# Seven products for a sixth pair of up chunks in each MLP, with sums of weight quarters made during attention

## The chip, the cores and the metric

One core of one Trainium2 chip runs one program. The metric is the device time of one execution in microseconds (us); lower is better. A profile of one execution gives the engines' instructions, their waits and the DMA packets. The engines are PE (TensorE, matmuls), DVE (VectorE), ACT (ScalarE), POOL (GpSimd) and SP (SyncE, which here only issues DMAs); a "q" behind a name is the engine's instruction queue.

## What is computed

A trunk of two layers works on 256 tokens of width 2048, all in float32. Layer 0 is causal attention with forget gates (FoX, 16 heads of 128), layer 1 is a mixture of three dilated windows (8 heads). Each mixer is followed by an MLP with a hidden width of 8192:

```
x = x + mixer(rms_norm(x) ; w_in, w_out)
h = rms_norm(x)
a = relu(h @ w_up)            # w_up 2048 x 8192
x = x + (a * a) @ w_down      # w_down 8192 x 2048
```

The weights, some 400 MB, are read from DRAM once in each run.

## The kernel before

**Matmuls.** To keep float32 accuracy, each operand is split into a rounded part `hi` and a rest `lo` (type fp32r), and each product is three matmuls (hi by hi, hi by lo, lo by hi; L447 to L449 in `product_steps`, L1138 to L1140 in `slot_steps`). A matmul is 128x128 by 128x512. A weight matrix is cut into chunks of 512 columns, and a chunk into row blocks of 128.

**A unit of weights.** Two row blocks of one chunk, 128x1024 floats or 512 KB, are one unit. SP loads it into one of five `raw` buffers (`load`, L373), ACT casts it to `wh` (L398), DVE subtracts to get `wl` (L399, both in `split_part`), and PE multiplies it with both halves of the tokens: 2 row blocks x 2 token tiles x 3 = 12 matmuls. There are five buffers of `wh` and five of `wl`, so units are split up to five ahead of PE. A raw buffer is loaded again when DVE has split its unit.

**The order.** Everything is written as coroutines in class `Jobs`. `product_steps` calls `jobs.tick()` behind each row block (a *step* below is one tick; one row block is 6 matmuls). A job that says `yield n` goes on n ticks later, `yield key` waits until that key is reached, and `clear(n)` is n or n+1 ticks, whichever ends on the right parity. The order in which instructions are written is the order in which each engine runs them; `pin` fixes it. So a chain is placed by counting ticks, and an engine that reaches an instruction too early waits there with all that is behind it.

**Stages.** FoX attention: 12 chunks of `fox_w_in`, then 4 of `fox_w_out`. MLP "n1". Dilated attention: 16 chunks of `dil_w_in`, 4 of `dil_w_out`. MLP "n3". During the attention chunks, heads run beside the products: `qk_chain` (norms, a transpose through DRAM blocks, scaling), `fox_head` and `dil_head` (scores, softmax, the transpose of the probabilities by `p_turned` through DRAM, `pv`).

**An MLP** has four blocks b of the hidden width, of four up chunks n each. `UP_ALONE` lists up chunks that are ordinary products; chunks 0 and 1 of block 0 are ordinary as well. Behind the up chunks of a block come its four down chunks. Counted in units of ordinary work, an MLP has 22 chunks x 8 = 176 units.

**Wide pairs.** The remaining up chunks go in pairs (b, n), (b, n+1) as 2x2 blocks: two row blocks by two chunks are four quarters B11, B12, B21, B22, the two token tiles by two row blocks are A11 to A22, and the product is formed with seven products in place of eight, by sums of quarters on both sides (`PRODUCTS`). The sums of tokens are made once for each MLP (`token_sums`). For each of the 8 pairs `pr` of row blocks, three *slots* are woven between ordinary units, and one more slot for two `pr` together:

- what 0, "crossed": the quarters off the diagonal, as they are (2 products, 6 matmuls)
- what 1, "differences": `sd` = crossed minus B22 (2 products)
- what 2, "sums": `v` (2 products)
- what 3, "rows": B21 of two `pr`, for the eighth matrix of partial sums (2 products for two `pr`)

Each slot is a unit of 512 KB that ACT casts and DVE subtracts as any other. DVE also makes `sd` and `v` (L395 128x1024; L401 and L402, 128x512 each) in `split_part`. Two loads of 512 KB feed slots 0 to 2, one load feeds a slot 3. `WIDE_AT` says behind which ordinary unit of the MLP each slot of each pair comes; a slot is also one tick. `wide_chain` then adds the six banks of partial sums (L1100 to L1109, one ACT copy and six DVE operations of 128x512), applies relu and square, and `turn_up` transposes through DRAM and splits into `aTh`, `aTl` (tags of four buffers each), which the down chunks read. Those two tags also hold the attention outputs `oT`.

The five pairs are (1,0), (2,0), (2,2), (3,0), (3,2).

Of the kernel before, what the change touches and what calls it, by code (L numbers as in the profile page):

```python
# [9 lines left out]
F32 = mybir.dt.float32  # L10
# [7 lines left out]
P = 128  # L18
D = 2048
S = 256  # L20
NT = S // P
NC = 512
# [97 lines left out]
def trunk(ctx: ExitStack, tc, x, fox_w_in, fox_b_f, fox_q_gain, fox_k_gain, fox_w_out, dil_w_in,  # L120
# [168 lines left out]

    def add_slot(w, c, what, pr):  # L290

        r = pr * RAW_SUB * P
        if what == 3:
            units.append((len(plan), "rows"))
            plan.append([((slice(0, RAW_SUB), slice(0, NC)),
                          w[r:r + 2 * RAW_SUB * P, c:c + NC].rearrange("(c q p) n -> p c q n", p=P, q=RAW_SUB)[:, :, 0])])
            return
        if what == 0:
            woven["at"] = len(plan)
            for first, by in ((0, NC), (NC, -NC)):  # L300
                corner = w[r:r + P, c + first:c + first + NC]
                rows, columns = corner.ap
                crosswise = bass.AP(corner.tensor, corner.offset, [rows, [rows[0] * P + by, RAW_SUB], columns])
                plan.append([((slice(0, RAW_SUB), slice(0, NC)), crosswise)])
        units.append((woven["at"] + 1, ("crossed", "differences", "sums")[what]))
# [17 lines left out]
    def add_mlp(l):  # L323
        woven["count"] = 0
        for at, (b, n, what, pr) in wide_slots():
            woven["due"].setdefault(at, []).append((mlp_w_up[l], b * D + n * NC, what, pr))
# [38 lines left out]
    def load():  # L365
        i = state["raw"]
        if i >= len(plan):
            return
        t = wpool.tile([P, RAW_SUB, NC], F32, tag="raw", name=f"raw{i}", bufs=RAW_BUFS)
        for (k, columns), src in plan[i]:  # L370
            hold(t)
            for rows in [slice(x, x + 1) for x in range(RAW_SUB)] if i == 1 else [None]:
                nc.sync.dma_start(t[:, k if rows is None else rows, columns], src if rows is None else src[:, rows])  # L373
        raws.append(t)
        state["raw"] += 1
# [39 lines left out]

    def in_turn(w, apart=NC // 2):
# [673 lines left out]
    def wide_chain(banks, tag, b, n, aT):  # L1092
# [34 lines left out]

    def slot_steps(tag, banks, what, pr, then):

        hi, lo = splits[used[0]]  # L1130
        for bank, i, a, of in [(0, i, 4, pr + i) for i in range(2)] if what == 3 else [(*x, pr) for x in PRODUCTS[what]]:
            wh, wl = (in_turn(w[:, i, :]) for w in (hi, lo))
            if a < 4:
# [13 lines left out]
    def mlp(tag, **after):  # L1147
        aTs = [{} for b in range(4)]
        banks = []

        def one(b, n, what, pr):
            if pr == 0 and what in (0, 2):
                pools = ((ps_acc, f"acc{1 - turn['only']}"),) if what else ((ps_tp, "tp"), (ps_sc, "sc"))
                banks[2 * what:] = [pool.tile([P, NC], F32, tag=of, name=f"wide_{tag}_{b}_{n}_{of}{i}")
                                    for pool, of in pools for i in range(2)]
# [9 lines left out]
            slot_steps(tag, banks, what, pr, then)  # L1165

# [95 lines left out]

    tag = "n0"
    for j in range(4):
        qT, kT = zip(*(heads_pairs(f"f{j}_{i}", i) for i in range(2)))
# [54 lines left out]
```

## Time and profile before

| | |
|---|---|
| median of 3 runs | 2084.48 us (2082.59 to 2084.88) |
| the profiled execution | 2084.9 us, its span 2083.2 us |
| PE busy / DVE busy / ACT busy | 2076.8 / 1714.9 / 1305.8 us |
| POOL busy | 275.2 us |
| DMA | 539.04 MB, mean 259 GB/s |
| core's granted TensorE clock | 1.00 |

The span runs from the first instruction to the last; the 1.7 us outside it are start and end of the execution. Busy time of an engine is the union of its instructions' durations. PE's matmuls are pipelined: a matmul that lasts 379 ns is followed by the next long before its end, so the pace is read from the starts, not from the durations. "DMA share" is the mean share of time in which packets were under way on the 16 DMA engines; packets that overlap on one engine can take it over 1.

### The profile page before, as it was taken

How to read it: one execution, taken by the hardware profiler on the slowest of the kernel's cores; microseconds unless marked ns; L12 is line 12 of the kernel's file. 1: busy time of each engine (PE TensorE's matmuls, PEld its weight loads, DVE VectorE, ACT ScalarE, POOL GpSimd, SP SyncE). 2: the span in 40 equal slices, each digit the busy share in tenths (PEclk: the TensorE clock that was granted, in tenths of full speed). 3: DMA queues.
4: the chain of work that ended last, by engine and by line, in shares of the span. 5: the costliest groups of instructions: out<-in, count | busy, mean ns of one | idle time of the engine just before them, and what ended most of it. 6: DMA issues, size and time to landing. Idle time of an engine off the chain costs nothing.

```text
span 2083.2 us, 28968 instructions
## 1 busy us (share of the span) xinstructions
PE 2076.8 (100%) x9835; PEld 1818.5 (87%) x9835; DVE 1714.9 (82%) x2183; ACT 1305.8 (63%) x1825; POOL 275.2 (13%) x398
## 2 busy tenths in 40 slices
PE   9999999999999999999999999999999999999999
PEld 7888888888888888888888888888888888888888
DVE  6888876898989889888668787766998898899874
ACT  6665654866666667564656565556766676666662
POOL 2000000011212111120010010000113031212120
PEclk9999999999999999999999999999999999999999
DMA  7888887888988898897877876877889888898885
GB/s 254 259 259 260 262 248 212 267 285 262 268 281 269 262 296 269 267 291 247 279 242 229 250 239 210 260 212 237 262 272 272 278 276 265 276 287 276 265 280 165
DMA packets 357205, 539.04 MB, mean 259 GB/s; under 512 B 43752, under 2 KB 144448, under 8 KB 357056
## 3 DMA queue, kind: packets, MB, share of 16 engines
q1 hardware_dynamic: 334624, 507.41, 76.8%
q0 software_dynamic: 22016, 29.38, 6.2%
q8 instruction: 77, 1.26, 0.3%
q10 hardware_dynamic: 416, 0.39, 0.1%
q14 instruction: 72, 0.59, 0.1%
HBM read 484.09 MB, written 40.39 MB: 252 GB/s over the span
## 4 chain that ended last, share of the span: by engine, by line
PE 97%; ACT 1%; DMA 1%; DVE 1%; issue 0%; SPq 0%; ACTq 0%; DVEq 0%
PE acc L448 26%; PE acc L447 26%; PE acc L449 25%; PE wide_n_tp L1139 2%; PE wide_n_tp L1140 2%; PE wide_n_tp L1138 2%; PE wide_n_sc L1139 2%; PE wide_n_acc L1140 2%; PE wide_n_acc L1139 2%; PE wide_n_sc L1140 2%; PE wide_n_sc L1138 2%; PE wide_n_acc L1138 2%; PE sc_d L798 0%; DMA raw<-in_fox_w_in_dram 0%; ACT room_n L552 0%; ACT wh L398 0%
## 5 line engine op out<-in xcount | busy, mean ns | idle before, releaser
L399 DVE TENSOR_TENSOR wl<-raw,wh 128x1024 fp32r<-128x1024 f32 (+1 forms) x763 | 919.5, 1214 | 308.5 <-ACT wh L398 299.3
L398 ACT CAST wh<-raw 128x1024 fp32r<-128x1024 f32 (+1 forms) x763 | 787.2, 1046 | 505.5 <-PE acc L449 368.7
L447 PE MATMUL acc<-wh,hT_n 128*128 128x512 f32 x1280 | 486.7, 380 | 0.4 <-ACT hT_n L628 0.2
L448 PE MATMUL acc<-wl,hT_n 128*128 128x512 f32 x1280 | 485.6, 379 | 0.5 <-DVE wl L399 0.5
L449 PE MATMUL acc<-wh,hT_n 128*128 128x512 f32 x1280 | 485.4, 379 | 0.0
L449 PEld LDWEIGHTS acc<-wh,hT_n 128*128 128x128 f32 x1280 | 241.9, 189 | 34.8 <-DVE hT_n L629 0.4
L448 PEld LDWEIGHTS acc<-wl,hT_n 128*128 128x128 f32 x1280 | 242.1, 189 | 34.6 <-DVE wl L399 2.1
L447 PEld LDWEIGHTS acc<-wh,hT_n 128*128 128x128 f32 x1280 | 242.1, 189 | 34.3 <-ACT hT_n L628 1.2
L447 PE MATMUL acc<-wh,aTh_n1a 128*128 128x512 f32 x512 | 194.0, 379 | 0.0
L448 PE MATMUL acc<-wl,aTh_n1a 128*128 128x512 f32 x512 | 194.0, 379 | 0.0
L449 PE MATMUL acc<-wh,aTl_n1a 128*128 128x512 f32 x512 | 194.0, 379 | 0.0
L447 PE MATMUL acc<-wh,aTh_n3a 128*128 128x512 f32 x480 | 181.9, 379 | 0.0
L448 PE MATMUL acc<-wl,aTh_n3a 128*128 128x512 f32 x480 | 181.9, 379 | 0.0
L449 PE MATMUL acc<-wh,aTl_n3a 128*128 128x512 f32 x480 | 181.9, 379 | 0.0
L994 POOL DMA_DIRECT2D x<-y_n x96 | 84.7, 1331 | 479.9 <-ACT y_n L993 421.4
L398 ACT CAST wh<-sd 128x1024 fp32r<-128x1024 f32 x80 | 84.1, 1051 | 99.4 <-DVE sd L395 77.6
L398 ACT CAST wh<-v 128x1024 fp32r<-128x1024 f32 x80 | 84.1, 1051 | 54.3 <-PE acc L449 42.7
L448 PEld LDWEIGHTS acc<-wl,aTh_n1a 128*128 128x128 f32 x512 | 96.8, 189 | 13.8
L447 PEld LDWEIGHTS acc<-wh,aTh_n1a 128*128 128x128 f32 x512 | 96.8, 189 | 13.7
L449 PEld LDWEIGHTS acc<-wh,aTl_n1a 128*128 128x128 f32 x512 | 96.8, 189 | 13.7
L449 PEld LDWEIGHTS acc<-wh,aTl_n3a 128*128 128x128 f32 x480 | 90.7, 189 | 12.9
L447 PEld LDWEIGHTS acc<-wh,aTh_n3a 128*128 128x128 f32 x480 | 90.7, 189 | 12.9
(665 smaller groups left out, 3227.7 us busy)
## 6 DMA issues: line engine op xcount, KB each, us to landing
raw<-in_mlp_w_up_dram SPq DMA_DIRECT2D x296, 512.0 KB, 4.9
raw<-in_mlp_w_down_dram SPq DMA_DIRECT2D x256, 512.0 KB, 5.0
raw<-in_dil_w_in_dram SPq DMA_DIRECT2D x192, 256.0 KB, 3.6
raw<-in_fox_w_in_dram SPq DMA_DIRECT2D x94, 512.0 KB, 4.7
raw<-in_fox_w_out_dram SPq DMA_DIRECT2D x32, 512.0 KB, 4.9
raw<-in_dil_w_in_dram SPq DMA_DIRECT2D x32, 512.0 KB, 5.4
raw<-in_dil_w_out_dram SPq DMA_DIRECT2D x32, 512.0 KB, 4.4
x<-y_n POOLq DMA_DIRECT2D x96, 128.0 KB, 6.4
```

The source lines that it names most:

```text
L398: nc.scalar.copy(hi[:, part, :], raw[:, part, :])
L399: nc.vector.tensor_sub(lo[:, part, :], raw[:, part, :], hi[:, part, :].bitcast(F32))
L447: nc.tensor.matmul(acc[t], ah[:, tok], hi, start=first, stop=False)
L448: nc.tensor.matmul(acc[t], ah[:, tok], lo, start=False, stop=False)
L449: nc.tensor.matmul(acc[t], al[:, tok], hi, start=False, stop=last)
L994: nc.gpsimd.dma_start(xt[n][:, t, h * HC:h * HC + HC], y, accum_op=ALU.add)
L1138: nc.tensor.matmul(banks[bank], ah, wh, start=what < 3 and of == 0, stop=False, **alone)
L1139: nc.tensor.matmul(banks[bank], ah, wl, start=False, stop=False, **alone)
L1140: nc.tensor.matmul(banks[bank], al, wh, start=False, stop=of == KC // 2 - 1, **alone)
```

## The change

Three things.

1. **A sixth pair.** (1,2) joins `WIDE`, `UP_ALONE[1]` becomes empty, and an MLP has 20 ordinary chunks, 160 units. `WIDE_AT` is written anew: the first pair's slots lie behind units 15 to 37, and from then on a pair begins every 18 units (39, 57, 75, 93, 111), its eight `pr` two units apart. Before, the pairs began at 15, 45, 71, 98 and 122.

2. **Sums ahead.** A new job, `sums_ahead(l, start)`, runs beside the attention chunks of its layer: for each (b, n, pr) in `AHEAD[l]` it loads crossed and diagonal quarters (two loads of 512 KB, on SP), makes the differences and the sums with four DVE operations (one 128x1024, three 128x512), and stores both to DRAM (`kept`, two stores of 512 KB, on POOL). `AHEAD[0]` has ten row block pairs (the eight of pair (1,0), one of (2,0), one of (3,0)); `AHEAD[1]` has sixteen (the eight of (1,0) and two each of (1,2), (2,0), (2,2), (3,0)). In the MLP, such a `pr` is three plain loads (crossed from the weights, both sums from `kept`), and DVE makes no `sd` and `v` for it. The work tiles are one buffer each of the tags `aTh` and `aTl`.

3. **The first copy of `wide_chain` moves.** The chain is now started when slot 0 of the last `pr` is done; it copies P1 at once and waits for a key, "pieces", reached behind slot 2 of the last `pr`. The banks are kept in a dictionary by pair.

```diff
-WIDE = ((1, 0), (2, 0), (2, 2), (3, 0), (3, 2))
-WIDE_AT = ((15, 19, 23, 27, 31, 34, 37, 39, 41, 42, 42, 43), (45, 47, 50, 53, 55, 58, 61, 63, 66, 67, 67, 68),
-           (71, 74, 77, 79, 82, 85, 87, 90, 93, 93, 94, 95), (98, 101, 103, 106, 109, 111, 114, 117, 119, 119, 120, 120),
-           (122, 125, 127, 130, 133, 135, 138, 141, 143, 143, 144, 145))
-UP_ALONE = ((2, 3), (2, 3), (), ())
+WIDE = ((1, 0), (1, 2), (2, 0), (2, 2), (3, 0), (3, 2))
+WIDE_AT = ((15, 18, 20, 23, 26, 28, 31, 33, 35, 36, 36, 37),
+           *(tuple(at + x for x in (0, 2, 4, 6, 8, 10, 12, 14, 15, 16, 16, 16)) for at in range(39, 112, 18)))
+AHEAD = tuple([(1, 0, pr) for pr in range(KC // 2)] + more for more in (
+    [(2, 0, 4), (3, 0, 0)], [(*pair, pr) for pair in WIDE[1:5] for pr in (2, 5)]))
+UP_ALONE = ((2, 3), (), (), ())
...
-    def add_slot(w, c, what, pr):
+    def add_slot(w, c, what, pr, ahead=None):
...
+        if ahead is not None:
+            units.append((len(plan), "rows"))
+            plan.append([(whole, (ahead, what - 1) if what else crosswise(w, r, c, -NC))])
+            return
...
+    def sums_ahead(l, start):
+
+        yield start
+        diagonal, crossed = (act.tile([P, RAW_SUB, NC], F32, tag=f"aT{x}", name=f"ahead_{l}_{x}", bufs=KC // 4) for x in "hl")
+        for i, (b, n, pr) in enumerate(AHEAD[l]):
+            at = mlp_w_up[l], pr * RAW_SUB * P, b * D + n * NC
+            move(crossed, crosswise(*at, -NC))
+            move(diagonal, crosswise(*at, NC))
+            yield clear(5)
+            first, second = (crossed[:, x, :] for x in range(2))
+            q11, q22 = (diagonal[:, x, :] for x in range(2))
+            nc.vector.tensor_sub(crossed, crossed, q22.unsqueeze(1).to_broadcast([P, RAW_SUB, NC]))
+            yield 1
+            nc.vector.tensor_add(q22, q22, first)
+            nc.vector.tensor_add(q22, q22, second)
+            yield 1
+            nc.vector.tensor_sub(q11, q11, q22)
+            kept[l, b, n, pr] = [dram.tile([P, RAW_SUB, NC], F32, tag=f"kept{x}", name=f"kept_{l}_{i}_{x}", bufs=sum(map(len, AHEAD)))
+                                 for x in range(2)]
+            nc.gpsimd.dma_start(kept[l, b, n, pr][0], crossed)
+            yield 1
+            nc.gpsimd.dma_start(kept[l, b, n, pr][1], diagonal)
+            yield 5
...
     def wide_chain(banks, tag, b, n, aT):
...
+        p1 = by_column(banks[0])
+        nc.scalar.copy(c12, p1)
+        yield (key, "pieces", n)
         p1, p3, p7, p5, p6, p4 = (by_column(x) for x in banks)
-        nc.scalar.copy(c12, p1)
-        yield 1
         nc.vector.tensor_sub(c12, c12, p6)
...
             def then():
+                if what == 0 and pr == KC // 2 - 1:
+                    jobs.spawn(wide_chain(banks, tag, b, n, aTs[b]))
                 if what == 2 and pr == KC // 2 - 1:
-                    jobs.spawn(wide_chain(list(banks), tag, b, n, aTs[b]))
+                    jobs.reach((f"{tag}a{b}", "pieces", n))
...
     tag = "n0"
+    jobs.spawn(sums_ahead(0, 20))
...
     mlp("n1", then=normed("n2", KC))
+    jobs.spawn(sums_ahead(1, 4))
     dilated("n2")
```

A `pr` made ahead has its two quarters the other way round in the buffer, which `slot_steps` takes into account (`turned`).

More of the change, by code (lines that the diff above doesn't have):

```diff
@@ L288, in add, with crosswise @@
             woven["count"] += 1
-    def add_slot(w, c, what, pr):
+    def crosswise(w, r, c, by):
+        corner = w[r:r + P, c + (0 if by > 0 else NC):c + (0 if by > 0 else NC) + NC]
+        rows, columns = corner.ap
+        return bass.AP(corner.tensor, corner.offset, [rows, [rows[0] * P + by, RAW_SUB], columns])
+    kept = {}
+    def add_slot(w, c, what, pr, ahead=None):
         r = pr * RAW_SUB * P
@@ L297, in add_slot @@
             return
+        whole = (slice(0, RAW_SUB), slice(0, NC))
+        if ahead is not None:
+            units.append((len(plan), "rows"))
+            plan.append([(whole, (ahead, what - 1) if what else crosswise(w, r, c, -NC))])
+            return
         if what == 0:
             woven["at"] = len(plan)
[L300 to L304, printed above, removed]
+            for by in (NC, -NC):
+                plan.append([(whole, crosswise(w, r, c, by))])
         units.append((woven["at"] + 1, ("crossed", "differences", "sums")[what]))
@@ L1126, in wide_chain, with slot_steps @@
         yield from turn_up(squared(first, tiles[1]), key, n, aT, (tag, "free", b - 1, n))
-    def slot_steps(tag, banks, what, pr, then):
+    def slot_steps(tag, banks, what, pr, then, turned=False):
         hi, lo = splits[used[0]]
         for bank, i, a, of in [(0, i, 4, pr + i) for i in range(2)] if what == 3 else [(*x, pr) for x in PRODUCTS[what]]:
-            wh, wl = (in_turn(w[:, i, :]) for w in (hi, lo))
+            wh, wl = (in_turn(w[:, 1 - i if turned else i, :]) for w in (hi, lo))
             if a < 4:
@@ L1159, in then @@
             def then():
+                if what == 0 and pr == KC // 2 - 1:
+                    jobs.spawn(wide_chain(banks, tag, b, n, aTs[b]))
                 if what == 2 and pr == KC // 2 - 1:
-                    jobs.spawn(wide_chain(list(banks), tag, b, n, aTs[b]))
+                    jobs.reach((f"{tag}a{b}", "pieces", n))
                 if what == 3 and pr == KC // 2 - 2:
                     jobs.reach((f"{tag}a{b}", "crossed", n))
-            slot_steps(tag, banks, what, pr, then)
+            slot_steps(tag, banks, what, pr, then, what == 2 and (b, n, pr) in AHEAD[int(tag == "n3")])
         jobs.spawn(token_sums(tag))
```

12 lines of the change are left out of this document (9 added, 3 removed).

## Prediction, before the run

> **What bounds the kernel now.** First the page: the span, the busy times, the chain that ended last.
>
> ```profile
> span 2083.2 us, 28968 instructions
> PE 2076.8 (100%) x9835; PEld 1818.5 (87%) x9835; DVE 1714.9 (82%) x2183; ACT 1305.8 (63%) x1825; POOL 275.2 (13%) x398
> PE 97%; ACT 1%; DMA 1%; DVE 1%; issue 0%; SPq 0%; ACTq 0%; DVEq 0%
> ```
>
> PE is idle for 2083.2 - 2076.8 = 6.4 us in all, so the time is the number of matmuls times their pace. The pace is in PE's timeline inside MLP n1 (the first of 16 matmuls in a row and the last):
>
> ```profile
> 699.67 0.38 PE L447 MATMUL acc<-wh,aTh_n1a 128*128 128x512 f32 x1
> ...
> 702.91 0.38 PE L1138 MATMUL wide_n_tp<-wh,hT_n 128*128 128x512 f32 x1
> ```
>
> 15 starts lie in 3.24 us: 0.216 us for each matmul, a step (6) is 1.30 us, an ordinary unit (12) 2.59 us. All that PE can gain is fewer matmuls; all that it can lose is waiting for an engine that now hides behind it. So the next views are the stages' windows (columns: length, then busy time of PE, PEld, DVE, ACT, POOL with counts, clock, DMA share, GB/s), of FoX, MLP n1 and dilated attention, then three short ones with much DMA:
>
> ```profile
> 50.00:250.00 200.00, 200.00 (x980) 176.56 (x979) 164.38 (x286) 119.37 (x194) 10.74 (x6) 1.00 0.85 258
> 517.00:918.00 401.00, 401.00 (x1859) 350.87 (x1858) 358.74 (x368) 264.67 (x318) 79.97 (x123) 1.00 0.88 274
> 1020.00:1340.00 320.00, 320.00 (x1557) 282.33 (x1556) 240.13 (x349) 190.19 (x278) 24.10 (x13) 1.00 0.79 242
> 10.00:20.00 10.00, 9.74 (x49) 7.82 (x50) 8.23 (x15) 7.07 (x15) 0.83 (x3) 1.00 1.05 393
> 915.00:945.00 30.00, 30.00 (x141) 26.27 (x140) 25.40 (x32) 20.05 (x27) 13.09 (x22) 1.00 0.97 310
> 620.00:640.00 20.00, 20.00 (x94) 17.50 (x94) 18.70 (x21) 15.39 (x21) 8.95 (x17) 1.00 0.95 317
> ```
>
> DVE is busy for 82% of FoX, 89% of the MLP's weave, 75% of the dilated stretch. ACT's largest share is 66%, so it has room. What DVE and the SP queue waited for says whether these are near their limits (us, times, longest; the first two rows are FoX, 28 to 228 us, the third is SP over the span):
>
> ```profile
> DVE wl L399 <- ACT wh L398: 29.9, 35, 1.9
> DVE bias L882 <- DMA bias<-negc: 3.1, 2, 2.5
> SPq L373 <- DVE wl L399: 804.9, 437, 4.9
> ```
>
> SP waits for a free raw buffer for 805 us: the loads run as fast as units are used up, so the rates of the windows above are demand, not a ceiling.
>
> **The change part by part.**
>
> *The sixth pair.* Two ordinary chunks are 2 x 16 row blocks x 2 token tiles x 3 = 192 matmuls. A wide pair is 8 `pr` x 3 slots x 6, and 4 slots of 6: 168. 24 are saved in each MLP, 48 in all, x 0.216 = **10.4 us off PE**. There is no cover here: PE is the path.
>
> *DVE in the denser weave.* What operations take on DVE when nothing holds them is read from start to start:
>
> ```profile
> 652.47 1.23 DVE L395 TENSOR_TENSOR sd<-raw,raw 128x1024 f32<-128x1024 f32 x1
> 653.61 1.22 DVE L399 TENSOR_TENSOR wl<-raw,wh 128x1024 fp32r<-128x1024 f32 x1
> 654.75 0.68 DVE L401 TENSOR_TENSOR v<-raw,sd 128x512 f32<-128x512 f32 x1
> 655.46 0.69 DVE L402 TENSOR_TENSOR v<-raw,v 128x512 f32<-128x512 f32 x1
> 656.07 1.22 DVE L399 TENSOR_TENSOR wl<-sd,wh 128x1024 fp32r<-128x1024 f32 x1
> 657.21 1.22 DVE L399 TENSOR_TENSOR wl<-raw,wh 128x1024 fp32r<-128x1024 f32 x1
> ```
>
> A 128x1024 is 1.14 us, a 128x512 is 0.71 in front of one that needs it and 0.61 otherwise. What one `pr` loses when it is made ahead (`sd` and two `v`) is 1.14 + 0.71 + 0.61 = 2.46 us. The window 517 to 918 holds these groups:
>
> ```profile
> L399 DVE TENSOR_TENSOR wl<-raw,wh 128x1024 fp32r<-128x1024 f32 x147 | 177.7, 1218 | 36.2 <-ACT wh L398 35.4
> L395 DVE TENSOR_TENSOR sd<-raw,raw 128x1024 f32<-128x1024 f32 x32 | 39.0, 1218 | 2.5 <-DMA raw<-in_mlp_w_up_dram 2.4
> ```
>
> 32 `sd` are four pairs; of the 147 raw units 32 are crossed and 16 slot 3, so 99 are ordinary. DVE's 358.74 us are then 99 x 1.14 and four times 61.5 us for a pair with its chains. In the new weave a pair has 18 ordinary units: DVE 18 x 1.14 + 61.5 = 82.0 us, PE (18 x 12 + 168) x 0.216 = 82.9. From unit 39 to 128 that is five pairs, 414.7 us of PE. In n1 two `pr` are ahead: DVE 5 x 82.0 - 2 x 2.46 = 405 us, 98%. In n3 eight are: 390 us, 94%. It fits, with 10 us to spare in n1, of which DVE's waits on DMA (2.4 us above) take a part. Up to five split units lie ahead of PE, 5 x 2.59 = 13 us, so an uneven stretch need not be seen. I take 1.5 us lost in n1 and 0.5 in n3; bounds 0 and 10 (the last worked out under the rivals). The first pair (units 15 to 37) has no sums to make in either MLP, so DVE is lighter there.
>
> *DMA in the MLP.* In 401 us at 274 GB/s 109.9 MB moved; the raw loads are 99 + 4 x 20 of 0.524 MB, 93.8 MB, and the rest 40 GB/s. New: 38 loads in a pair's 82.9 us, 240, one or two more for `kept`, and the rest: 286 to 293 GB/s. The first pair has 22 + 28 loads in 93 us: 281 + 40 = 321 GB/s, just over what the 20 and 30 us windows show and far under 393. At 310 it would be 3 us late, which the 13 us of lead hide: 0, bounds 0 and 3.
>
> *Sums ahead, DVE.* In one turn: 1.14 + 0.71 + 0.71 + 0.61 = 3.2 us (3.3 by the durations). A turn is 5 or 6, 1, 1, 1 and 5 ticks, 14 as a rule. How long a step is in FoX: the loads issued between 50 and 250 us.
>
> ```profile
> raw<-in_fox_w_in_dram SPq DMA_DIRECT2D x73, 512.0 KB, 4.5
> DMA to landing us min/median/max: 2.7/4.8/9.4
> ```
>
> 73 units, 146 steps in 200 us, 1.37 us each; a turn is 19.2 us and the ten turns are 192 us, from step 20 to 160 of 192, ahead of the last group's `oT`, which takes the buffer back. DVE's idle time there is 35.6 of 200, 34.2 of 192; 32 to 33 are needed. **This is the tightest place: 99%**, and the 3.1 us that DVE waits for `bias` are part of the idle. At the harshest, only the idle time in which DVE waited for ACT (29.9 us of 200, 28.7 of 192) can be filled, and 33 us are needed: 4.3 too much, which the lead of 13 us covers. A turn's loads have 6.9 to 8.2 us until DVE wants them; raw loads land in 4.8 us, at worst 9.4, so 0 to 2.5 us more in a turn. I take 1 us lost in FoX, bounds 0 and 16 (4.3 + 25 - 13). In the dilated stretch DVE has 79.9 us idle of 320 and sixteen turns need 51 to 53 us: 0, bounds 0 and 10, by the landings alone.
>
> *Sums ahead, DMA.* Four transfers of 0.524 MB in 19.2 us are 109 GB/s more: 258 + 109 = **367 GB/s in FoX for 192 us**, 242 + 109 = 351 in the dilated stretch for 307 us. Nothing in the trace holds such a rate for so long; 393 holds for 10 us, 317 for 20, 310 for 30, the last two by demand. The new packets are as large as those of the weights or larger, so the 10 us row is the nearest: I take no loss, and the other end is a rival.
>
> The Trainium skill, "DMA: Bandwidth & Descriptors", section Bandwidth, puts the HBM limit for each core at about 358 GB/s and says that this side binds between HBM and SBUF. By it FoX's 70.5 MB would need 197 us in place of 192, 5 us more, inside the lead unless DVE has spent it; the sum would then be up to 5 us worse. The trace has 393 GB/s for 10 us on this core, over that figure, so I don't take it.
>
> *POOL.* 52 stores are issued there. What an issue costs:
>
> ```profile
> L994 POOL DMA_DIRECT2D x<-y_n x96 | 84.7, 1331 | 479.9 <-ACT y_n L993 421.4
> L1050 POOL DMA_DIRECT2D held_n1a<-turned_n1a x128 | 70.5, 559 | 182.6 <-DVE turned_n1a L1056 181.2 <-issue 1.2
> ```
>
> 0.56 us for 64 KB, 1.33 for 128 KB of 128 rows; 512 KB of 128 rows is between 0.56 and four times 1.33; I take 1.33, since the rows are as many. POOL is 5% busy in FoX. A store waits for the DVE operation written just before it; behind it on POOL is the power of `qk_chain`, which has four ticks (5.5 us): 0. On SP, a turn's first load waits for the last turn's stores to leave the buffer, with raw loads behind it; the stores have 5 ticks, 6.9 us, and the raw buffers a lead: 0, up to 2 us in a turn, inside the bounds above.
>
> *The copy of P1* moves three slots forward on ACT, and holds a buffer of tag "w" longer: 0. The gap from one pair's last slot to the next pair's first is two units; before it was two or three (43 to 45, 120 to 122) with PE never idle: 0, at worst a unit (2.6 us) for each of ten gaps. The chunk boundaries (15, 23, 31 and so on to 127), where PE must wait for ACT to read a bank, still each have a slot behind them: 0.
>
> **The sum.** 2084.9 - 10.4 + 1.5 + 0.5 + 1 = 2077.5 for an execution like the profiled one; the median of before is 0.4 lower, so **2077.0**.
>
> **Rivals.**
>
> *The DMA engines don't keep up beside attention (slower).* If the ceiling for long is the 317 of the 20 us row, FoX's 70.5 MB take 222 us and the dilated stretch's 107.8 MB 340 us: 30 and 33 more than PE needs, less 13 us of lead each, 37 lost: 2084.5 - 10.4 + 37 = 2111. It outweighs the gain where the ceiling is under some 333 GB/s ((178.3 MB) / (499 + 26 + 10.4 us)). For it: no long window is faster, and the share is already 0.97 at 310. Against: SP's 805 us of waiting for buffers, and the 393. Chance 0.19.
>
> *DVE takes the place of PE (no change).* The lead isn't there when it is wanted: FoX's 4.3 us are all lost, and each pair's end is too dense: two ordinary units, four slots and the six chain operations are 6 x 1.14 + 6 x 0.7 = 11.0 us of DVE beside 2 x 2.59 + 4 x 1.30 = 10.4 of PE, 0.6 us for ten pairs. 10.3 lost: 2084.4; with half of that 2079.3. For it: 98 and 99%. Against: five units of lead, and the weave before ran at 89% without one idle stretch of PE. Chance 0.15.
>
> *The change gives nothing of what it says*, since the banks or the `aT` buffers are not free for a pair that begins 18 units after the last: 10 gaps x 2.6 = 26 us, 2100. The trace had gaps as short. Chance 0.04.
>
> **How the numbers follow.** The forecast has 0.62: between 2074.1 (no loss) and 2080. A measurement of this kernel tells 0.2%, 4.2 us, from no change, so "faster" ends at 2080.3 and "slower" begins at 2088.7. Of the DVE rival 0.02 lies below, 0.13 between; of the DMA rival 0.04 is mild enough to lie between, 0.15 is slower, and so are the 0.04 of the last. Faster 0.64, same 0.17, slower 0.19. The range goes from 2073.5 to 2094: the forecast, the DVE rival and the milder half of the DMA rival, with some 0.15 left out above.
>
> **What would show it.** Right: PE with 48 fewer 128x512 matmuls and still under 9 us idle; DVE near 97% busy between units 39 and 128 of n1 and 98% in FoX; GB/s near 360 beside attention. DMA rival: `wh` on ACT waits for raw loads in FoX, landings of 8 us and more, PE idle before `acc`. DVE rival: PE waits for `wl` in n1 and FoX, and DVE's wait for `wh` is gone. I am wrong altogether if PE's pace itself changes, or if POOL's larger stores hold up the power behind them.

## The result, and the profile after

The changed kernel takes **2181.1 us** (median of four runs, 2174.7 to 2183.8), the kernel before 2084.2 (2082.6 to 2084.9): a ratio of 1.0462, 95% interval 1.0436 to 1.0487. It is 97 us slower; 10.4 us of matmuls did go, so some 107 us were lost elsewhere. The profiled execution is one of 2183.8.

First the page: the span, busy times, the chain that ended last, and the DMA total.

```profile
span 2182.0 us, 29393 instructions
...
PE 2106.1 (97%) x9787; PEld 1824.5 (84%) x9787; DVE 1800.7 (83%) x2293; ACT 1331.0 (61%) x1853; POOL 306.7 (14%) x450
...
DMA packets 381432, 611.43 MB, mean 280 GB/s; under 512 B 45960, under 2 KB 146656, under 8 KB 381280
...
PE 57%; DMA 15%; DVE 13%; issue 8%; ACT 4%; SPq 2%; POOL 1%; DVEq 0%; ACTq 0%; POOLq 0%
```

48 matmuls are gone, and PE has the path for 57% of the span in place of 97%. Two losses are to be read here. PE is idle for 2182.0 - 2106.1 = 75.9 us, 69.5 more than before. And PE is *busy* 29.3 us longer with 48 matmuls fewer, so the matmuls that are left took nearly 40 us more.

Where: the first and last start of the products that end each stage (the rows of the tiles `oTfh`, `aTh_n1a`, `oTdh`, `aTh_n3a`), before and then after.

```profile
L447 PE MATMUL acc<-wh,oTfh x128: 379/379/382, 278.6 to 365.3; 128*128 128x512 f32 x128
L447 PE MATMUL acc<-wh,aTh_n1a x512: 379/379/379, 468.3 to 1004.0; 128*128 128x512 f32 x171
L447 PE MATMUL acc<-wh,oTdh x128: 379/379/382, 1352.9 to 1440.7; 128*128 128x512 f32 x128
L447 PE MATMUL acc<-wh,aTh_n3a x480: 379/379/379, 1542.6 to 2057.6; 128*128 128x512 f32 x160
```

```profile
L485 PE MATMUL acc<-wh,oTfh x128: 379/379/382, 305.3 to 392.0; 128*128 128x512 f32 x128
L485 PE MATMUL acc<-wh,aTh_n1a x512: 379/379/634, 502.3 to 1044.8; 128*128 128x512 f32 x171
L485 PE MATMUL acc<-wh,oTdh x128: 379/379/382, 1440.5 to 1528.3; 128*128 128x512 f32 x128
L485 PE MATMUL acc<-wh,aTh_n3a x480: 379/379/742, 1637.8 to 2156.8; 128*128 128x512 f32 x160
```

FoX, up to the first `oTfh`, takes 26.7 us longer. MLP n1, from the last `oTfh` to the last `aTh_n1a`, goes from 638.7 to 652.8, +14.1; with the 5.2 us of matmuls gone that is 19.3 lost. Dilated attention, up to the first `oTdh`, goes from 348.9 to 395.7, +46.8. n3 goes from 616.9 to 628.5, +11.6, 16.8 lost. Attention lost 73.5, the MLPs 36.1. The next sections give each run's differences by these four marks.

What PE waited for in the whole span (us in all, times, longest):

```profile
PE sc_d L833 <- DVE sd L969: 15.1, 4, 5.4
PE acc L485 <- ACT y_n L1031: 10.9, 8, 2.0
PE acc L486 <- DVE wl L413: 10.5, 11, 3.0
PE sc_f L836 <- DVE f_0kl L754: 8.4, 2, 5.7
PE po_f L785 <- DVE pT_f L813: 7.8, 5, 4.1
```

The scores (`sc_d`, `sc_f`) and the products with the probabilities (`po_f`) stall in attention, not the weights' products; in the MLPs it is `acc`, on ACT's reading of a bank (`y_n`) and on `wl`. DVE in its turn stood for the loads of its own sums, in all and once in the dilated stretch:

```profile
DVE ahead_l L443 <- DMA ahead_h<-in_mlp_w_up_dram: 57.2, 18, 8.1
```

```profile
1167.61 1.23 DVE L443 TENSOR_TENSOR ahead_l<-ahead_l,ahead_h 128x1024 f32<-128x1024 f32 x1 [6.02 <-DMA ahead_h<-in_mlp_w_up_dram]
```

Two windows answer to those of before (FoX and dilated), and four short ones surround one stall in MLP n1, whose matmuls follow in the timeline:

```profile
50.00:250.00 200.00, 181.03 (x846) 156.57 (x845) 166.28 (x278) 103.97 (x169) 21.20 (x23) 0.96 0.95 316
...
1020.00:1340.00 320.00, 294.85 (x1349) 253.99 (x1348) 250.02 (x367) 168.39 (x259) 32.19 (x36) 0.96 0.92 299
```

```profile
794.00:797.90 3.90, 3.90 (x19) 3.40 (x19) 2.50 (x4) 3.80 (x5) 2.88 (x6) 1.00 0.90 326
...
800.40:804.90 4.50, 4.20 (x12) 3.39 (x13) 4.46 (x6) 2.53 (x3) 2.07 (x4) 0.62 0.84 241
```

```profile
800.71 0.61 PE L486 MATMUL acc<-wl,aTh_n1a 128*128 128x512 f32 x1 [2.39 <-DVE wl L413]
...
802.39 0.63 PE L487 MATMUL acc<-wh,aTl_n1a 128*128 128x512 f32 x1
802.81 0.63 PE L485 MATMUL acc<-wh,aTh_n1a 128*128 128x512 f32 x1
```

FoX moved 316 GB/s, not the 367 expected. The granted clock, 1.00 in every window of before, is 0.96 in both attention windows. At 802 us two matmuls start 0.42 us apart in place of 0.216: half speed, for some 3.4 us behind a stall of 2.39 us. So a stall can be paid again in the pace behind it. After has 13 stretches with a granted clock of 0.50, each 3.41 or 6.83 us long, 65 us together; PE is busy for 53 of these, and half of that, 27 of the nearly 40 us, is an estimate of what the pace costs. The rest is not worked out here; a matmul in front of a stall counts as busy for its whole 0.38 us and not for 0.216, which is a part of it. The Trainium skill, "TensorE: Matmul & The Clock Gate", Part 1, says that an activity monitor halves the clock by windows of about 3.4 us; the length and the factor agree with these figures.

### The profile page after: what moved, and what is told of

Same layout as the page of the kernel before. It is cut to its first block, busy times and chain, and to the rows that moved or that the text cites. A ratio compares the mean times of both kernels' runs of the same rounds, so it can differ in the third digit from the quotient of the medians.

```text
span 2182.0 us, 29393 instructions
## 1 busy us (share of the span) xinstructions
PE 2106.1 (97%) x9787; PEld 1824.5 (84%) x9787; DVE 1800.7 (83%) x2293; ACT 1331.0 (61%) x1853; POOL 306.7 (14%) x450
## 4 chain that ended last, share of the span: by engine, by line
PE 57%; DMA 15%; DVE 13%; issue 8%; ACT 4%; SPq 2%; POOL 1%; DVEq 0%; ACTq 0%; POOLq 0%
PE acc L485 14%; PE acc L486 14%; PE acc L487 14%; DVE wl L413 6%; DMA raw<-in_dil_w_in_dram 4%; DMA ahead_h<-in_mlp_w_up_dram 2%; ACT wh L412 2%; DMA raw<-in_mlp_w_up_dram 2%; PE wide_n_tp L1179 1%; PE wide_n_tp L1178 1%; PE wide_n_tp L1177 1%; PE wide_n_sc L1178 1%; PE wide_n_sc L1179 1%; PE wide_n_sc L1177 1%; PE wide_n_acc L1178 1%
## 5 line engine op out<-in xcount | busy, mean ns | idle before, releaser
L413 DVE TENSOR_TENSOR wl<-raw,wh 128x1024 fp32r<-128x1024 f32 (+1 forms) x807 | 971.9, 1214 | 260.0 <-ACT wh L412 253.4
L412 ACT CAST wh<-raw 128x1024 fp32r<-128x1024 f32 (+1 forms) x807 | 833.8, 1045 | 551.0 <-PE acc L487 316.8
L485 PE MATMUL acc<-wh,hT_n 128*128 128x512 f32 x1152 | 444.6, 386 | 4.4 <-DVE dv0hl L764 2.7
L486 PE MATMUL acc<-wl,hT_n 128*128 128x512 f32 x1152 | 443.9, 385 | 5.0 <-DVE wl L413 4.8
L487 PE MATMUL acc<-wh,hT_n 128*128 128x512 f32 x1152 | 442.4, 384 | 0.0
L486 PEld LDWEIGHTS acc<-wl,hT_n 128*128 128x128 f32 x1152 | 221.8, 193 | 39.5 <-DVE wl L413 9.1
L485 PEld LDWEIGHTS acc<-wh,hT_n 128*128 128x128 f32 x1152 | 222.1, 193 | 36.6 <-DVE dv0hl L764 3.1
L487 PEld LDWEIGHTS acc<-wh,hT_n 128*128 128x128 f32 x1152 | 221.2, 192 | 32.4 <-DVE hT_n L667 0.4
L412 ACT CAST wh<-sd 128x1024 fp32r<-128x1024 f32 x70 | 73.5, 1050 | 82.2 <-DVE sd L409 77.2
L486 PEld LDWEIGHTS acc<-wl,aTh_n3a 128*128 128x128 f32 x480 | 91.7, 191 | 17.9 <-DVE wl L413 5.1
L487 PEld LDWEIGHTS acc<-wh,aTl_n3a 128*128 128x128 f32 x480 | 91.8, 191 | 13.1
```

The costliest lines, as they stand in the source:

```text
L412: nc.scalar.copy(hi[:, part, :], raw[:, part, :])
L413: nc.vector.tensor_sub(lo[:, part, :], raw[:, part, :], hi[:, part, :].bitcast(F32))
L485: nc.tensor.matmul(acc[t], ah[:, tok], hi, start=first, stop=False)
L486: nc.tensor.matmul(acc[t], ah[:, tok], lo, start=False, stop=False)
L487: nc.tensor.matmul(acc[t], al[:, tok], hi, start=False, stop=last)
```

## Experiments on attention

All runs below were timed against the kernel before on the same chip. The four differences are those of the stages above (FoX, n1, dilated, n3), in the profiled execution, so their sum can be some us off the median (5 in a_spread, 6 in a_loads). Losses in the text are medians less that of the kernel before in the same comparison. The first four take `sums_ahead` apart: the kernel before, with the job alone (its sums used by nothing), then without its DVE operations, without its DMAs, without its stores.

```diff
@@ before -> a_full: sums_ahead as in the change, and
+    jobs.spawn(sums_ahead(0, 20))
+    jobs.spawn(sums_ahead(1, 4))
@@ a_full -> a_dma: the four DVE operations out
-            nc.vector.tensor_sub(crossed, crossed, q22...)
-            nc.vector.tensor_add(q22, q22, first)
-            nc.vector.tensor_add(q22, q22, second)
-            nc.vector.tensor_sub(q11, q11, q22)
@@ a_full -> a_dve: both move() and both stores out (memset once ahead)
@@ a_full -> a_loads: both stores out
-            nc.gpsimd.dma_start(kept[l, b, n, pr][0], crossed)
-            nc.gpsimd.dma_start(kept[l, b, n, pr][1], diagonal)
```

> The kernel before with the job sums_ahead of the change beside attention (10 and 16 turns), its stored sums used by nobody; the MLPs are those of before. If the attention stretches of the changed kernel lose their time by the job alone (+26.7 us to the first matmul of fox_w_out, +46.8 us in the dilated input chunks), this is 2084 + 73 = 2157 us, with the granted clock under 1. If part of it came from the changed MLPs (work left over, other buffers), it is less: 2084 to 2140.

> The same job with its four DVE operations left out: what it loads it stores unchanged, nobody uses it; the transfers (two loads and two stores of 512 KB in a turn) stay. Transfer theory (DMA engines near their ceiling, landings late, chains and weights wait): nearly all of the full job's loss stays, 2084 + 50 to 73. DVE theory (3.2 us more DVE work in a turn of 19 us): 2084 + 0 to 10. My prediction put FoX's loss at 1 us and the transfers' at none.

> The same job with its loads and stores left out: the four DVE operations of each turn run on two buffers that are zeroed once. Transfer theory: 2084 + 0 to 8. DVE theory: 2084 + 50 to 73. The sum of my prediction (DVE at 99% in FoX, 5 split units of lead) gives + 1 us.

> The full job without its two stores in a turn: loads and DVE operations stay, half of the added bytes goes (about 55 GB/s more in place of 109), and SP no longer waits for stores to leave the buffers. If the rate is what counts (ceiling near 320 GB/s, demand 313 in FoX and 297 in the dilated stretch), 2084 + 0 to 20. If DVE's in-order wait for the landing of its own loads is what counts, the loss stays: 2084 + 40 to 70.

| run | median us | ratio, 95% interval | FoX, n1, dilated, n3 |
|---|---|---|---|
| a_full | 2153.8 | 1.0332 [1.0317, 1.0348] | +28.7, +1.5, +42.0, -0.3 |
| a_dma | 2122.1 | 1.0179 [1.0162, 1.0196] | +14.5, 0.0, +21.9, +0.2 |
| a_dve | 2099.3 | 1.0070 [1.0055, 1.0085] | +11.1, +0.2, +4.6, -0.3 |
| a_loads | 2138.6 | 1.0262 [1.0244, 1.0280] | +25.6, -1.3, +35.9, -0.2 |

The job costs 69 us by itself, nearly the whole loss of the attention stages. Its transfers alone cost 37, DVE's operations alone 14; the sum is 51, so 18 come only when both are there. Loads with DVE cost 54, more than loads and stores without DVE. Neither theory on record holds alone: the 37 and the 14 both lie between what the two had foreseen.

The windows 56 to 240 (FoX) and 1050 to 1300 us (dilated) show how each is lost; before, then a_dma, then a_dve:

```profile
56.00:240.00 184.00, 184.00 (x901) 162.38 (x901) 149.25 (x249) 112.04 (x183) 10.74 (x6) 1.00 0.86 261
```

```profile
56.00:240.00 184.00, 172.46 (x834) 150.19 (x833) 136.46 (x227) 102.63 (x168) 20.80 (x23) 1.00 0.99 336
1050.00:1300.00 250.00, 238.39 (x1122) 207.02 (x1121) 178.01 (x255) 139.03 (x199) 31.70 (x34) 0.97 0.97 326
```

```profile
56.00:240.00 184.00, 175.82 (x843) 152.97 (x842) 166.33 (x269) 104.67 (x173) 10.91 (x5) 0.99 0.82 246
```

In a_dma the DMA engines are busy for 99% at **336 GB/s**. FoX's 70.5 MB then take 210 us in place of 192, 18 more, and 14.5 were lost; the dilated stretch's 107.8 MB at 326 take 331 in place of 307, 24 more, and 21.9 were lost. Hardly anything of the lead of 13 us is seen. What PE waited for in a_dma says why:

```profile
PE sc_d L825 <- DVE sd L961: 7.5, 2, 6.7
PE po_f L777 <- DVE pT_f L805: 5.8, 5, 2.2
PE sc_f L828 <- DVE f_0kl L746: 4.9, 3, 2.6
PE acc L478 <- DVE wl L409: 2.8, 6, 0.8
```

The units' products (`acc`) wait 2.8 us, the heads' three rows 18.2. A head's chain has transfers of its own between its instructions (`turned_f`, `bias`, the blocks); these land later in the full engines. From 20 to 300 us, DVE and ACT stand for two of them in a_dma:

```profile
DVE bias L912 <- DMA bias<-negc: 15.6, 8, 6.7
ACT pT_f L803 <- DMA turned_f<-pblocks_f: 18.5, 6, 4.3
```

In before these rows have 3.3 and 0.2 us. Five split units are no lead for a score that PE must run in its written place. In a_dve DVE is busy for 90%, not 99%, and still 11.1 us are lost in FoX: an average under 100% doesn't say that each chain's operation comes in time.

Next, whether bytes, order, bursts or DVE's waits for its own loads carry this.

```diff
@@ a_dma -> a_dma_small: an eighth of the bytes, the same issues
-            move(crossed, crosswise(*at, -NC))
+            move(crossed[:, :, 0:64], crosswise(*at, -NC)[:, :, 0:64])    (and so on for the other three)
@@ a_dma -> a_spread: each transfer in two pieces of 256 KB, at ticks of their own
+            for t, x, src in pieces:
+                move(t[:, x, :], src)
+                yield 2
@@ a_loads -> a_lonly: the DVE operations out as well
@@ a_loads -> a_loads_early: twice the ticks from the loads to DVE
-            yield clear(5)
+            yield clear(10)
...
-            yield 5
+            yield 0
@@ a_full -> a_slack, before -> c_slack: two ticks more in each head's chain
-        yield clear(6)          (qk_chain)
+        yield clear(8)
-        yield clear(landing)    (p_turned)
+        yield clear(landing + 2)
```

> The transfers alone (a_dma, + 37), each cut to 64 of its 512 columns: as many DMAs, in the same places of the SP and POOL queues and with the same waits for landings, and an eighth of the bytes. Byte theory (rate, and other transfers landing later behind these): 2084 + 0 to 8. Queue theory (SP stands at a load until the last turn's store has left the buffer, with the weights behind it): 2084 + 25 to 37.

> The kernel before, with the job's loads and stores alone (no DVE operations; the stored values are not sums and used by nothing), each cut into two pieces of 256 KB at ticks of their own, two to four ticks apart, in place of a megabyte at once. The bytes are the same. Rate theory: no change against the run with whole transfers, 2122 (+37 us over the kernel before), GB/s 330 to 336 in FoX. Burst theory (a megabyte in front of the weights' loads holds these up, and the engines have room in between): 2094 to 2104 (+10 to +20).

> The kernel before, with the two 0.5 MB loads of each turn of the attention job alone: no DVE operations, no stores, so the loaded values are used by nothing. Demand is then 258 + 54 = 312 GB/s in FoX and 242 + 54 = 296 in the dilated stretch. Rate theory (the transfers cost time only where their bytes exceed what the engines moved for long, 327 to 336 GB/s in the run with loads and stores): 0 to 5 us over the kernel before, 2084 to 2089. Contention theory (loads slow the weights' landings well below that rate): about half of the 37 us of loads and stores, 2098 to 2106. If the rate theory holds, the 54 us of loads with DVE operations are not bytes but DVE's order: 14 of DVE's time and some 35 to 40 of DVE standing at its own loads.

> Of the kernel before with loads and DVE operations beside attention and no stores (53.7 us slower than before), with the loads issued 10 or 11 ticks ahead of the first DVE operation in place of 5 or 6, at the same 13 to 14 ticks in a turn. Landing theory (DVE stands 59 us waiting for its own loads, since ticks pass faster than at PE's pace when DVE is the one that is late): 2084 + 15 to 30, about the DVE operations alone (14) and something for the bytes. Rate theory: unchanged, 2084 + 54.

> The kernel before with the full job beside attention (2153.8), and two more ticks in each chain between the read back from DRAM and its first use (in qk_chain 8 or 9 in place of 6 or 7, in p_turned two more behind the read). Work, bytes and order of the loads are the same. Chain theory (PE waits for scores and products with values whose transposes through DRAM land late; the five split units ahead of PE do not help those): a good part goes, 2105 to 2140. Rate theory (DMA engines full): unchanged, 2145 to 2155.

> The control of a_slack: the kernel before with two more ticks in the chains and no job beside attention. If the ticks alone cost nothing, 2084 to 2088, and a_slack's 2170 says that more slack does not help the chains. If the ticks alone cost more than the 16 us by which a_slack is over a_full, the job costs less with slack than without (69), and the chain theory stands in part.

| run | median us | ratio, 95% interval | FoX, n1, dilated, n3 |
|---|---|---|---|
| a_dma_small | 2084.5 | 1.0002 [0.9993, 1.0011] | -1.2, -0.4, 0.0, -0.3 |
| a_spread | 2104.8 | 1.0093 [1.0077, 1.0110] | +15.8, -0.1, +9.5, -0.3 |
| a_lonly | 2094.9 | 1.0053 [1.0038, 1.0068] | +6.0, -0.3, +4.5, -0.1 |
| a_loads_early | 2125.8 | 1.0194 [1.0179, 1.0209] | +19.1, -1.1, +22.8, -0.3 |
| a_slack | 2170.0 | 1.0405 [1.0389, 1.0420] | +40.1, +0.3, +40.9, -0.2 |
| c_slack | 2090.0 | 1.0029 [1.0018, 1.0040] | +0.5, -1.0, +0.5, -0.3 |

*Bytes, not issues.* With an eighth of the bytes and every issue in its place, nothing is lost: the issues on SP and POOL are not the cause. FoX's weights land 4.5 us after their issue in before, 5.1 here and 6.4 in a_dma (medians, 56 to 240 us). A queue that stands because a transfer ahead of it lands late goes with the bytes, and no run separates it from them.

*Rate and bursts.* The two theories of a_spread are each right for one stage. Its windows:

```profile
56.00:240.00 184.00, 173.49 (x828) 151.10 (x827) 135.28 (x225) 102.63 (x168) 29.55 (x39) 0.98 1.00 335
1050.00:1300.00 250.00, 245.19 (x1173) 215.29 (x1172) 180.08 (x257) 144.17 (x209) 46.28 (x61) 0.99 1.00 339
```

FoX stays at 335 GB/s and loses as much as with whole transfers: there the rate fits as the limit. The dilated stretch goes from 326 to 339 and its loss from 21.9 to 9.5, near the 11 us that 107.8 MB at 339 take beyond 307 (318): the rest there went with the transfers of a whole megabyte at one place.

*Loads alone* are dearer than the rate theory allows (+10.6 at 305 and 291 GB/s, shares of 0.94 and 0.91; 0 to 5 expected) and cheaper than the contention theory's 14 to 22.

*Loads and DVE together.* 10.6 for the loads and 14 for the operations leave about 29 of a_loads's 54. With the loads issued earlier, DVE's row for its own loads falls from 59.3 us in a_loads to 1.9, and the loss from 53.7 to 41.7, by 12. So 12 of the 29 were DVE standing in front of the sums with the heads' work behind it. That is less than the landing theory had foreseen, which put the loss at 15 to 30. Some of the other 17 is PE's pace: its busy time is 17.7 us over that of before in a_loads (granted clock 0.993), 1.7 in a_lonly (1.00) and 4.1 in a_dve (0.999). How the remainder divides stays open.

*Slack in the chains* fell as a theory: two more ticks cost 5.8 us without the job (c_slack), and with it the job costs 80 rather than 69. More ticks didn't help here; that ticks are instructions and not time, so that an engine which is late runs through them sooner, would explain it, and was not tested.

## Experiments on the MLPs

Each has the new weave and no job in attention, so that the MLPs stand alone; without any loss the time would be 2084.2 - 10.4 = 2073.8. A `pr` that is made ahead still has three loads in m_nojob, but of the raw quarters in place of the sums; m_noahead makes every sum in the MLP as before; m_allahead loads raw quarters for all 48 `pr`, so that DVE makes no sum; m_lean loads the crossed quarters of a `pr` once and splits that one buffer anew for each of its three slots.

```diff
@@ after -> m_nojob: both jobs.spawn(sums_ahead(...)) out, and
-            plan.append([(whole, (ahead, what - 1) if what else crosswise(w, r, c, -NC))])
+            plan.append([(whole, crosswise(w, r, c, -NC))])
@@ after -> m_noahead
+AHEAD = ((), ())
@@ m_nojob -> m_allahead, m_lean
+AHEAD = ([(*pair, pr) for pair in WIDE for pr in range(KC // 2)],) * 2
@@ m_lean only
+            if what == 0:
+                woven["at"] = len(plan)
+                plan.append([(whole, crosswise(w, r, c, -NC))])
+            units.append((woven["at"], "rows" if what == 2 else "held"))
```

> The changed kernel without the job beside attention: in the MLPs the made-ahead row block pairs load the crossed quarters from the weights three times in place of the stored sums (same bytes, same instructions, so those products are not the reference's). Attention is that of before. Traces: n1 lost 19.3 us and n3 16.8 against the 10.4 us of fewer matmuls, so 2084.5 - 10.4 + 36 = 2110 if the MLPs lose by themselves; 2074 to 2078 if their loss was carried over from attention.

> The sixth pair and the new weave, nothing made ahead: DVE makes all sums in the MLPs, in each 48 row block pairs x 2.46 us = 20 to 39 us more DVE work than m_nojob. DVE-amount theory: the loss grows by about that in each MLP where DVE has no idle time left (2110 + 30 to 60). Pair-end theory (ACT and DVE wait for each other around the end of one pair and the begin of the next): little more, 2110 to 2120.

> As m_nojob, but all 48 row block pairs of each MLP are plain loads, so DVE makes no sums there at all (62 us in a pair's 83). DVE-amount theory: the loss is gone, 2074 to 2078. Pair-end theory: what waits at the pairs' ends (y behind the chain's activations, 1.95 us at four chunk boundaries, and the clock after it) stays: 2082 to 2095. Loads rise to 3.5 for each row block pair: were the DMA engines the limit in the MLP, it would be slower than m_nojob.

> As m_allahead (2107.9, DMA share 0.97 in the weave), but the three slots of a row block pair all use the one load of crossed quarters (so those products are not the reference's): DVE makes no sums and the raw loads of a pair fall from 28 to 12. If m_allahead lost by the DMA engines and m_nojob by DVE's work, so that each alone is harmless, this is 2074 to 2080. If the ends of pairs 18 units apart cost time by their order alone (ACT, DVE and PE waiting in turn), 2085 to 2105.

| run | median us | ratio, 95% interval | over 2073.8 | FoX, n1, dilated, n3 |
|---|---|---|---|---|
| m_noahead | 2123.5 | 1.0188 [1.0172, 1.0203] | 50 | +0.8, +20.5, 0.0, +18.3 |
| m_nojob | 2113.8 | 1.0140 [1.0123, 1.0157] | 40 | +0.5, +12.9, 0.0, +15.1 |
| m_allahead | 2107.9 | 1.0117 [1.0102, 1.0132] | 34 | +0.8, +10.3, +0.1, +10.7 |
| m_lean | 2093.8 | 1.0046 [1.0031, 1.0061] | 20 | +0.4, +5.9, +0.1, +4.2 |

The weave alone is slower than the kernel before, by 30 us in m_nojob; with a_full's 69 that makes 99, and the change measured 97: **the two halves add up**. The windows of m_nojob, m_allahead and m_lean from 518 to 929 us:

```profile
518.00:929.00 411.00, 401.95 (x1838) 346.60 (x1838) 380.82 (x393) 271.86 (x322) 72.83 (x109) 1.00 0.88 273
```

```profile
518.00:929.00 411.00, 401.31 (x1839) 346.99 (x1838) 302.81 (x284) 273.83 (x321) 70.13 (x104) 1.00 0.97 319
```

```profile
518.00:929.00 411.00, 404.39 (x1853) 351.42 (x1852) 302.20 (x286) 275.87 (x329) 71.50 (x107) 0.99 0.75 223
```

DVE falls from 380.8 to 302.8 us, a fifth less, and 6 us are won, though with 46 GB/s more; at the same DVE and 96 GB/s less, 14. With DVE at 74% and the DMA engines at 75%, 20 us are still lost: neither sum of work explains the other half of the loss. m_noahead makes the sums of 26 more `pr` on DVE than m_nojob, an estimated 26 x 2.46 = 64 us, and loses 10 us more. Neither theory had m_noahead's time (2110 to 2120, or 2140 and more) or m_allahead's (2074 to 2078, or 2082 to 2095); m_lean's lies in the pair-end theory's 2085 to 2105. The stalls lie in few places, most of them the same in these four runs. After, at the end of the second pair (ACT's timeline, then PE's):

```profile
611.28 2.47 ACT L1154 ACTIVATE c_n1a<-c_n1a 128x512 f32<-128x512 f32 x4 [4.08 <-DVE c_n1a L1147]
613.66 1.55 ACT L1031 ACTIVATE y_n<-acc,rstd_n 128x256 f32<-128x256 f32 x4
615.09 2.00 ACT L412 CAST wh<-raw 128x1024 fp32r<-128x1024 f32 x2
```

```profile
614.53 0.48 PE L485 MATMUL acc<-wh,aTh_n1a 128*128 128x512 f32 x1 [1.95 <-ACT y_n L1031]
```

The pair's last three slots all come at unit 55, which also ends a chunk. ACT has the pair's `c` ahead of `y` in its order and stands 4.08 us for DVE, which needs the last slots; then four activations, then `y`, and only then may PE write the bank: 1.95 us idle. Behind it the casts are late by as much. A pair ends so at units 55, 73, 91, 109 and 127 here; chunks end at 55 and 127 among these. A stall of 1.95 us on `y_n` stands at the first and the last in both MLPs, in after, m_nojob and m_lean. The longest in n1 of after (2.39 us, quoted above) lies behind the fourth pair: `wl` is written late behind four operations of `turn_up` on DVE. At the same place of n3 it is 2.98 us.

If packing the pairs is the cause, it must cost without a sixth pair: m_packed is the kernel before with five pairs, the last four packed into 17 units each. Their spacing is 24 to 28, as before on average.

```diff
-           (...45 to 68), (...71 to 95), (...98 to 120), (...122 to 145)
+           *(tuple(at + x for x in (0, 2, 4, 6, 8, 10, 12, 14, 15, 16, 16, 16)) for at in (51, 79, 103, 127)))
```

(The copy of P1 is early as in the change, so the run alone doesn't separate it from the packing. At the stalls, ACT stands 4.09 us for the additions on DVE behind the last slots, as above, and not at that copy.)

> The kernel before with its five pairs, all sums made by DVE in the MLP, no sixth pair and nothing ahead; the last four pairs are packed as in the changed kernel (slots at 0, 2, ... 14, 15, 16, 16, 16 from units 51, 79, 103 and 127, so 24 to 28 units from pair to pair as before, with eight or more ordinary units between them). Average-density theory: 2084 to 2089 (one chunk boundary, at unit 71, has no slot behind it). Packing theory (what happens within the 17 units is too much, and the units between do not make it good): eight pairs lose some 2 to 4 us each, 2100 to 2115.

Measured 2111.0, 1.0125 [1.0110, 1.0140]: +27, n1 +11.5 and n3 +14.0, with PE's waits:

```profile
PE acc L446 <- ACT y_n L992: 12.3, 8, 2.0
```

Its pairs end at 67, 95, 119 and 143; the last three end a chunk too, and there, three times in each MLP, is the same stall of 1.95 us. Adding up over n1 by how much each matmul's start lies later than 0.216 us behind the one before gives 13.0 us (1.6 in before); 10.1 of them lie within 8 us of these three pair ends. So the packed end of a pair is dear without a sixth pair, 2.3 to 3.9 us where it meets a chunk's end. The meeting alone is not: in before, the pair that begins at 71 ends at 95 too, with no stall, but there the last slot that the additions wait for lies four units ahead of the chunk's end, in m_packed one.

Three runs then changed the order at the end of a pair in m_nojob: ACT's activations three ticks later, the slots spread evenly, and both.

```diff
@@ m_late
-        yield clear(1)
+        yield clear(4)
@@ m_spread
-(0, 2, 4, 6, 8, 10, 12, 14, 15, 16, 16, 16)
+(0, 1, 3, 5, 6, 8, 10, 12, 13, 14, 15, 16)
```

> m_nojob (2113.8) with one size changed: the activations of a finished pair come 4 or 5 ticks behind the last of its additions in place of 1 or 2 (so its products are not the reference's either). Pair-end theory: ACT no longer stands 2 to 4 us before them with y and the casts behind it; the 1.95 us at four chunk boundaries go, and some of the clock's low time: 2100 to 2107. DVE-amount theory: no change, 2114.

> m_nojob with the same slots in the same 17 units, laid otherwise: the eight row block pairs in 13 units (0, 1, 3, 5, 6, 8, 10, 12) and the last four slots at 13, 14, 15 and 16 in place of 15, 16, 16, 16. Counts, bytes and DVE's work are the same. Pair-end theory (what loses is the dense end: four slots beside six additions, eight activations and four splits): 2095 to 2108. If it is the average density that loses, 2114; the denser row block pairs ahead of the end could also make it worse, up to 2125.

> m_late and m_spread together. Pair-end theory: at most what each gives, 2085 to 2100; no loss left would be 2073.8.

| run | median us | ratio, 95% interval | FoX, n1, dilated, n3 |
|---|---|---|---|
| m_late | 2129.0 | 1.0214 [1.0199, 1.0230] | -0.2, +20.8, 0.0, +23.7 |
| m_spread | 2124.8 | 1.0193 [1.0176, 1.0210] | -0.4, +18.4, 0.0, +21.9 |
| m_both | 2118.9 | 1.0170 [1.0154, 1.0185] | -0.8, +13.1, 0.0, +21.3 |

All three are slower than m_nojob's 2113.8: misses. The stalls of 1.95 us at the two chunk ends are gone in m_late and m_spread (1.56 us are left at the first in m_both), and others came. In m_late DVE stands 3.7 and 3.9 us for the block that `turn_up` sends through DRAM, and PE 4.43 and 4.65 us behind it, and the late activations stand in front of a later chunk's `y` (2.96 and 2.98 us). In m_spread `y` comes 4.54 us late behind the third pair's activations. So the place is shown, a remedy isn't; pairs that start a unit later, so that none ends with a chunk, were not tried. No version beat the kernel before.

## Why the prediction was wrong

It said 2077.0, with 0.64 for faster and a range up to 2094; it is 2181.1. By its steps:

- **Matmuls, -10.4: right.** 9787 in place of 9835.
- **DVE in the denser weave, 1.5 and 0.5 us: wrong**, 19.3 and 16.8. "It fits, with 10 us to spare" compared sums of busy time. m_lean lost 20 us with DVE at 74%. What counts is the order at a pair's end: PE's last slots, DVE, ACT, then the bank.
- **"The chunk boundaries ... still each have a slot behind them: 0": wrong.** At 55 and 127 a pair ends there and `y` stands behind its `c` on ACT: 1.95 us of idle PE each time.
- **DMA in the MLPs: 0 was too little.** 14 us lie between m_allahead and m_lean, at 319 and 223 GB/s; after runs at 273 between these, and how much of the 14 holds there no run shows. The first pair's window, the worry of that step, shows no stall over 1.1 us.
- **Sums ahead on DVE, 1 us: wrong**, 14 alone (11.1 in FoX, inside the bound of 16, and 4.6 in the dilated stretch, bound 10), and some 29 more together with the loads. The time that the loads have was worked out as ticks times 1.37 us. DVE stood for its loads 57.2 us in after, and issuing them earlier gave back 12 in a_loads_early. A late DVE, whose instructions lie closer in time than the ticks say, would explain it.
- **Sums ahead on the DMA engines, 0: wrong**, 37. "The 10 us row is the nearest" was the choice that failed: 393 GB/s for 10 us says how fast a burst goes, and 326 to 339 is what this mix held for long. The Trainium skill's limit of 358 ("DMA: Bandwidth & Descriptors", section Bandwidth), which the prediction set aside, is nearer, and still over what was held; an estimate by it has FoX's bytes 5 us late, and 14.5 were lost.
- **The lead of 13 us, which covered four of these steps: wrong.** It covers weights' units. The heads' products and a bank that is read late are not behind it: of the PE waits in a_dma 2.8 us are on units.
- **POOL, 0: right.** a_dma issues the stores of 512 KB in 0.58 and 0.54 us (medians), under the 1.33 that was taken, and a_dma_small, with as many issues, lost nothing.
- **"If PE's pace itself changes"** was named as what would overthrow the forecast, without a price. It did: PE was busy nearly 40 us longer than its matmuls should take, an estimated 27 of them at half speed.

The DMA rival (2111) had the right mechanism in attention: less the gain that it kept, its loss of 37 is that of a_dma. It came so near through two errors, a ceiling of 317 where 336 was held and a lead that isn't there. The DVE rival had the right place, a pair's end, at 0.6 us for a pair; the MLPs lost 36.1 in ten, 3.6 each if all of it is put there. The last rival's wait, for a bank of the next pair, is in no row of PE's waits in after. None of the cases joined the first two, and none had DVE in front of its own loads.

## What to carry to other kernels

A lead covers only what is queued behind it: before counting on it, ask of each product on the critical engine which chain feeds it, and whether that chain passes through the resource to be filled. A job that loads for its own operations on an in-order engine must be placed by the time that its loads need when that engine is late, and a packed stretch is to be judged at the ends where its chain meets another one's buffer, not by its mean. For a rate to be held over 200 us, take the longest windows as evidence and leave the burst aside.

## What the runs showed of the hardware

Half speed in PE comes with stalls. Each of the 13 stretches in after begins within a stall of 1.95 us or more or at most 1.0 us behind it; before, whose longest stall is 1.5 us, has none after its first 5 us. The length of a stall does not decide it alone: of the four of 1.95 us in after, those that end at 960.77 and 1749.04 us were followed by a clock of 0.50 for 3.41 us, those at 614.53 and 2095.11 were not, and neither were the 3.16 us in m_nojob (from 772 us). The Trainium skill, "TensorE: Matmul & The Clock Gate", section "HAM oscillation", asks for no idle gap over about 3.4 us; the 1.95 and the 2.39 (quoted above) show that shorter ones can do it. And the DMA engines, at a share of 0.97 to 1.00 with small and large packets mixed, moved 326 to 339 GB/s on this one core (319 in m_allahead's MLP), where 393 had been seen over 10 us in before.
